# Two chained blocks on one core: weight rests on VectorE, smaller convolution pieces, an earlier bias product and a merged row scaling

## The chip, the cores and the metric

The kernel runs on one core of one Trainium2 chip. The metric is the time of one execution in microseconds (us); lower is better. Runs are summed up by their median.

## The reference

256 tokens of width 1024 go through two blocks, all in fp32. Cut to what matters here:

```
def first_block(x, ...):
    h = rms_norm(x, norm_mix_pre)
    u = h @ w_in
    o_nsa = nsa_attention(...)     # compressed, selected and window branches, with a relative bias table
    o_conv = short_conv_mixer(...)
    x = x + rms_norm(concat([o_nsa, o_conv]) @ w_out, norm_mix_post)
    h = rms_norm(x, norm_ffn_pre)
    y = (gelu(g) * up) @ w_ffn_down          # g, up: causal convolution (3 taps) of h @ w_ffn_up
    return x + rms_norm(y, norm_ffn_post)

def second_block(x, ...):
    h = concat([meta, x])                    # 16 + 256 rows
    z = rmsnorm(h, g_mix) @ w_in
    y_a = conformer_conv(conv_val, conv_gate, ...)   # 31 taps on 512 channels, layer norm, silu, @ w_conv_out
    y_b = rwkv7_mix(rwkv_in, ...)                    # a recurrence over time, 8 heads of 64, @ w_rwkv_out
    h = h + (gate_a * y_a + gate_b * y_b) @ w_o
    h = h + peer_ffn(rmsnorm(h, g_ffn), w_q, sub_keys, expert_u, expert_v)
    return rmsnorm(h, g_final)[:, N_META:]
```

## The kernel before

**Weights.** Every product is made of three matmuls (`mm3`, L371) of operands that are split into a high part and a rest. A weight tile of 128x1024 comes by a DMA on SyncE's queue into one of four `raw` buffers. ScalarE writes its high part into one of three `hl` buffers (`split`, L363); then the rest, raw minus high, is written at L364, on VectorE, or on GpSimd where the tile's `pool` flag is set in `front_tiles`. A raw buffer is free for the next load when its rest is written. `POOL1` and `POOLC` set the flag for two tiles of the first projection and four of the compression weights, and the line for `w_in_2` sets it for 35 of the 38 tiles of the second block's input projection.

**Opening** (`front_setup`, `start`, `bias_tables`). For each of two tiles of 128 rows a chain `a` or `b` makes the root of the mean square (`newton`, L421 to L429, on one number per partition), scales the rows by it and by g_pre (L797), turns them by eight TensorE transposes (L383) and splits them into hT (L805 on ScalarE, L808 on VectorE). The string `START` gives the order by hand on TensorE, VectorE, ScalarE and GpSimd: each letter takes chain a, chain b, the bias table (`t`) or a weight split (`s`) one step on.

**Boundaries** (the function around L540). Between parts the rows are normed again, in two chains: GpSimd multiplies the rows by the norm's weights (L540, two halves), `newton` runs on VectorE, and VectorE scales the product (L545, two halves); transposes follow. The steps' order is given by hand (`BORD`, `BORD1`, `BORD3`).

**Block 2.** Three generators are mixed into one TensorE order at build time. `rw`, the recurrence in five chunks of 64, sets the pace. `fill` gives projections of the next columns, so that TensorE has work while the recurrence goes through VectorE. `cf` is the conformer's convolution: four groups of 128 channels with 31 taps (L1250, L1252) on VectorE, then mean and variance by TensorE products with `cst`, the norm, the sigmoid and the split into cT. A `yield` after six taps ends a piece. The loop hands out a piece when the planned TensorE time since the start has passed CFP nanoseconds per piece given:

```
while ("U", min(ncf // 5, 3)) in emitted and (self.pe - base) > CFP * ncf:
    base = base or self.pe
    next(cf, None)
    ncf += 1
```

The products that use cT (w_conv_out) come after the recurrence. From then on block 2 has the merge with the recurrence's output oT, and after about 690 us the PEER part and the last norm follow; the change does not touch these.

Of the kernel before, what the change touches and what calls it, by code (L numbers as in the profile page):

```python
# [10 lines left out]
F32 = mybir.dt.float32  # L11
# [10 lines left out]
D = 1024  # L22
# [13 lines left out]
QUAD, PAIR = 150, 20  # L36
START = "abasabsbtasbt"
BT = (1, 2, 2, 2)
# [5 lines left out]
AC, AS, AX_, AP, AP0 = 1600, 1600, 1300, 1900, 2000  # L44
FILL0, FILL1, FILL2, CFP = 4500, .85, .7, 4900
SIDE = 2850
# [84 lines left out]
def front_tiles():  # L131

    t = []
# [52 lines left out]
    for i, c in enumerate(WIN2_ORDER):  # L186
        col("w_in_2", c, i < 3 or i >= 6)
    for name in ("w_conv_out_2", "w_rwkv_out_2"):
# [21 lines left out]
WIN_ORDER = [512, 640, 0, "k0", "k1", 128, "k2", "k3", 256, 384, 768, "v0", "v1", 1024]  # L210
POOL1 = (0, 1)
POOLC = ("k0", "k1", "v0", "v2")
for _i in range(2):
# [128 lines left out]
class Kern:  # L342
# [160 lines left out]
    def boundary(self, ys, g_post, g, hT, off, order=(0, 1), steps=BORD, lead=None, rest=None):  # L503
# [16 lines left out]
        def chain(tt):  # L520
# [17 lines left out]
            t = rows("xg")  # L538
            for c in cols:
                nc.gpsimd.tensor_mul(t[:, c], x[:, c], g[:, c])  # L540
            yield
            r = self.newton(s2, 1e-6, D)
            yield
            for c in cols:
                nc.vector.tensor_scalar(t[:, c], t[:, c], r, None, op0=OP.mult)  # L545
            parts = []
            for q in range(2):
                p = self.pb()
# [273 lines left out]
    def block1(self, ctx):  # L822
# [3 lines left out]
        self.tmp = tmp_ctx.enter_context(tc.tile_pool(name="tmp", bufs=1))  # L826
        self.g_pre = self.tmp.tile([128, 1024], F32, name="g_pre")
        nc.scalar.dma_start(self.g_pre, flat(A["norm_mix_pre"], 0, [[0, 128], [1, D]]))
        nc.scalar.dma_start(self.ident, A["cst0"])
        self.tab = self.tmp.tile([33, 8], F32, name="tab")  # L830
        nc.scalar.dma_start(self.tab, A["tab"])
        self.ohd = self.tmp.tile([33, NU], F32, name="ohd")
        nc.scalar.dma_start(self.ohd, A["ohd"])
        self.st.load()
        hT = self.turned("hT1")
# [348 lines left out]
    def block2(self, ctx):  # L1184
# [62 lines left out]
        def conformer():  # L1247
            acc = unit("acc", [128, 4, 256])
            for i in range(4):
                nc.vector.tensor_scalar(acc[:, i], UU[:, i, 46:302], self.v("cw", 120 + i), self.v("cb", i), op0=OP.mult, op1=OP.add)  # L1250
                for j in range(30):
                    nc.vector.scalar_tensor_tensor(acc[:, i], UU[:, i, 16 + j:272 + j], self.v("cw", 4 * j + i), acc[:, i],  # L1252
                                                   op0=OP.mult, op1=OP.add)
                    if j % 6 == 5:
                        yield
# [55 lines left out]
        while True:  # L1311
# [12 lines left out]
            while filled < target and fill_step():  # L1324
                pass
            while ("U", min(ncf // 5, 3)) in emitted and (self.pe - base) > CFP * ncf:
                base = base or self.pe
# [722 lines left out]
```

## Time and profile before

| | |
|---|---|
| median of 3 runs | 1519.92 us (1517.75 to 1520.23) |
| the profiled execution | 1517.68 us |
| its span, first to last instruction | 1515.9 us |
| mean granted TensorE clock | 0.978 of full speed |
| TensorE busy | 1433.8 us, 95% of the span |
| VectorE busy | 1067.5 us, 70% |
| ScalarE busy | 806.8 us, 53% |
| GpSimd busy | 282.5 us, 19% |

The profile is of one execution. Its own time stands beside the span, since sums over the trace are made against it and not against the median. PE is TensorE, DVE is VectorE, ACT is ScalarE, POOL is GpSimd, SP is SyncE; a q behind a name is the engine's queue of issues. A share of busy time is a mean over stages with different limits, so a stage is read by itself.

### The profile page before, as it was taken

To read this page: it belongs to the slowest core of one execution; us is meant where nothing else is said; L and a number is where in the kernel's file an instruction comes from. 1 tells how busy PE (TensorE), PEld (TensorE's weight loads), DVE (VectorE), ACT (ScalarE), POOL (GpSimd) and SP (SyncE) were. 2 spreads that over 40 slices of the span, in tenths; PEclk is the share of its full clock that TensorE was granted. 3 is DMA by queue.
4 is the path that set the end of the run, shared out by engine and by line. 5 is a ranking of instruction groups with operands and counts; after the bars stand their busy time and mean duration, and the time that the engine had idled before them with its cause. 6 is when DMAs were issued, how large, how long until landed. Compare 5 with 4: busy or idle time off the path is not lost.

```text
span 1515.9 us, 29516 instructions
## 1 busy us (share of the span) xinstructions
PE 1433.8 (95%) x11884; PEld 1312.1 (87%) x11884; DVE 1067.5 (70%) x1980; ACT 806.8 (53%) x1282; POOL 282.5 (19%) x143
## 2 busy tenths in 40 slices
PE   5999999997988789998999999999999999999997
PEld 4898899995877779988999899999999998888886
DVE  6877787777489974956970798874555556666666
ACT  4756565554662445544545577664444445555554
POOL 4100400005353423036786100000000000000000
PEclk9999999998998899999999999999999999999999
DMA  5634365554332112454576544457555558777773
GB/s 204 232 127 144 105 216 178 184 191 163 104 112 86 63 66 67 161 175 160 182 230 205 171 161 157 160 171 221 189 185 190 188 188 284 242 241 242 242 243 124
DMA packets 93024, 263.50 MB, mean 174 GB/s; under 512 B 10271, under 2 KB 34975, under 8 KB 92760
## 3 DMA queue, kind: packets, MB, share of 16 engines
q1 hardware_dynamic: 77200, 243.80, 49.0%
q10 hardware_dynamic: 15688, 17.83, 3.4%
q8 instruction: 93, 1.52, 0.4%
q14 instruction: 43, 0.35, 0.1%
HBM read 247.67 MB, written 13.91 MB: 173 GB/s over the span
## 4 chain that ended last, share of the span: by engine, by line
PE 75%; DVE 17%; ACT 4%; issue 2%; DMA 1%; POOL 1%; ACTq 0%; DVEq 0%; POOLq 0%
PE pb L371 39%; PE py L371 35%; DVE acc L1252 4%; DVE hl L364 2%; ACT hl L363 1%; PE pb L383 1%; DMA raw<-in_ws_dram 1%; POOL hl L364 1%; DVE m L1874 1%; DVE nc L425 0%; DVE blk L736 0%; DMA x<-in_x_dram 0%; ACT junk L515 0%; DVE nc L427 0%; DVE nc L426 0%
## 5 line engine op out<-in xcount | busy, mean ns | idle before, releaser
L371 PE MATMUL pb<-hT,hl 128*128 128x256 f32 (+1 forms) x4944 | 625.0, 285 | 9.4 <-DVE qT L364 4.0
L371 PEld LDWEIGHTS pb<-hT,hl 128*128 128x128 f32 x4944 | 607.2, 191 | 17.3 <-issue 5.1
L363 ACT ACTIVATE hl<-raw 128x1024 fp32r<-128x1024 f32 x412 | 434.1, 1054 | 231.4 <-issue 162.9
L364 DVE TENSOR_TENSOR hl<-raw,hl 128x1024 fp32r<-128x1024 f32 (+1 forms) x317 | 389.4, 1229 | 111.0 <-ACT hl L363 110.5
L371 PE MATMUL py<-hl,coef 128*128 128x512 f32 x1536 | 356.3, 390 | 0.0
L371 PEld LDWEIGHTS py<-hl,coef 128*128 128x128 f32 x1536 | 285.6, 188 | 59.3 <-ACT coef L363 0.3
L364 POOL TENSOR_TENSOR hl<-raw,hl 128x1024 fp32r<-128x1024 f32 x95 | 237.0, 2501 | 335.1 <-ACT hl L363 319.1
L1927 ACT ACTIVATE act<-pb 128x256 f32<-128x256 f32 x128 | 49.2, 384 | 166.2 <-PE pb L371 166.0
L2006 POOL TENSOR_TENSOR end<-end,end 128x512 f32<-128x512 f32 x2 | 2.6, 1278 | 664.6 <-DVE end L2004 663.1
L371 PE MATMUL py<-hT,hl 128*128 128x272 f32 (+1 forms) x768 | 118.1, 304 | 1.6 <-POOL hl L364 1.6
L371 PEld LDWEIGHTS py<-hT,hl 128*128 128x128 f32 x768 | 103.4, 198 | 8.3 <-issue 4.8
L364 DVE TENSOR_TENSOR coef<-act,coef 128x256 fp32r<-128x256 f32 x128 | 54.1, 423 | 72.3 <-ACT coef L363 72.3
L1931 DVE TENSOR_TENSOR act<-act,G 128x256 f32<-128x256 f32 x128 | 53.8, 420 | 34.1 <-ACT act L1927 33.2
L1252 DVE SCALAR_TENSOR_TENSOR acc<-UU,vt,acc 128x256 f32<-128x256 f32 x120 | 75.6, 671 | 0.7
L1887 ACT ACTIVATE G<-py 128x512 f32<-128x512 f32 x64 | 67.3, 1141 | 3.0 <-PE py L371 3.0
L1874 DVE TENSOR_TENSOR m<-e,gg 128x1536 bf16<-128x1536 bf16 x64 | 60.6, 954 | 0.7
L371 PE MATMUL py<-m,e 128*128 128x128 bf16 x768 | 52.7, 219 | 1.0 <-DVE m L1874 0.9
L363 ACT ACTIVATE coef<-act 128x256 fp32r<-128x256 f32 x128 | 51.6, 403 | 2.9 <-DVE act L1931 2.9
L1870 DVE TENSOR_TENSOR e<-gi,iota 128x1024 bf16<-128x1024 bf16 x64 | 43.7, 688 | 12.5 <-PE py L371 12.4
L371 PEld LDWEIGHTS <-e 128*128 128x128 bf16 x768 | 44.2, 97 | 4.5 <-DVE m L1874 2.5
L371 PE MATMUL py<-hl,gu 128*128 128x512 f32 x192 | 47.4, 393 | 0.4 <-DVE hl L364 0.3
L371 PEld LDWEIGHTS py<-hl,gu 128*128 128x128 f32 x192 | 34.9, 188 | 7.7 <-DVE hl L364 0.6
(419 smaller groups left out, 1358.6 us busy)
## 6 DMA issues: line engine op xcount, KB each, us to landing
raw<-in_ws_dram SPq DMA_DIRECT2D x172, 512.0 KB, 3.4
raw<-in_ut_dram SPq DMA_DIRECT2D x128, 512.0 KB, 3.4
raw<-in_ev_dram SPq DMA_DIRECT2D x128, 512.0 KB, 4.2
ad<-act ACTq DMA_DIRECT2D x90, 128.0 KB, 3.1
act<-ad SPq DMA_DIRECT2D x90, 128.0 KB, 3.0
wf<-fd ACTq DMA_DIRECT2D x2, 800.0 KB, 4.4
x<-in_x_dram SPq DMA_DIRECT2D x2, 512.0 KB, 5.9
xd<-x ACTq DMA_DIRECT2D x1, 1024.0 KB, 4.2
```

What stands on the lines that cost most here:

```text
L363: self.nc.scalar.activation(h, src, AF.Copy)
L364: (eng or self.nc.vector).tensor_sub(l, src, h.bitcast(F32))
L371: self.nc.tensor.matmul(out, lhsT, rhs, start=start, stop=stop, skip_group_check=True)
L383: self.nc.tensor.transpose(out, in_, self.ident[p0:p0 + n, p0:p0 + n])
L1252: nc.vector.scalar_tensor_tensor(acc[:, i], UU[:, i, 16 + j:272 + j], self.v("cw", 4 * j + i), acc[:, i], op0=OP.mult, op1=OP.add)
L1870: nc.vector.tensor_tensor(e.rearrange("p c a i j -> p (c a) i j"), gi[:, b].rearrange("p c (a j) -> p (c a) j", j=2)[:, :, None, :].to_bro ...
L1874: nc.vector.tensor_mul(m, e[:, 0][:, None].to_broadcast([128, 3, 2, 128, 2]), gg[:, b].rearrange("p k (a j) -> p k a j", j=2)[:, :, :, Non ...
L1887: nc.scalar.activation(G[:, :, 4 * b:4 * b + 4].rearrange("p a t -> p t a"), p.rearrange("p (t a) -> p t a", t=4), AF.Copy)
L1927: nc.scalar.activation(a, p[:, :S], AF.Gelu)
L1931: nc.vector.tensor_mul(a, a, self.G[:, c])
L2006: nc.gpsimd.tensor_mul(t[:, tt], x[:, tt, cols[1]], g[:, cols[1]])
```

## The change

1. `START` becomes another string, and the small loads of `tab` and `ohd` are issued ahead of `g_pre` and `ident` on ScalarE's queue. The bias table's products go ahead of the transposes.
2. `POOL1` and `POOLC` are empty and `w_in_2` carries no flag: 41 rests go from GpSimd to VectorE.
3. At the boundaries GpSimd's product and VectorE's scaling become one VectorE operation per half, x times r times g.
4. The conformer yields after every second tap (15 pieces for a group of channels instead of 5), and CFP goes from 4900 to 2300.

```
-START = "abasabsbtasbt"
+START = "abtabsababsts"
...
-FILL0, FILL1, FILL2, CFP = 4500, .85, .7, 4900
+FILL0, FILL1, FILL2, CFP = 4500, .85, .7, 2300
...
-        col("w_in_2", c, i < 3 or i >= 6)
+        col("w_in_2", c)
...
-POOL1 = (0, 1)
-POOLC = ("k0", "k1", "v0", "v2")
+POOL1 = ()
+POOLC = ()
...
             t = rows("xg")
-            for c in cols:
-                nc.gpsimd.tensor_mul(t[:, c], x[:, c], g[:, c])
             yield
             r = self.newton(s2, 1e-6, D)
             yield
-            for c in cols:
-                nc.vector.tensor_scalar(t[:, c], t[:, c], r, None, op0=OP.mult)
             parts = []
-            for q in range(2):
+            for q, c in enumerate(cols):
+                nc.vector.scalar_tensor_tensor(t[:, c], x[:, c], r, g[:, c], op0=OP.mult, op1=OP.mult)
...
-        self.g_pre = self.tmp.tile([128, 1024], F32, name="g_pre")
-        nc.scalar.dma_start(self.g_pre, flat(A["norm_mix_pre"], 0, [[0, 128], [1, D]]))
-        nc.scalar.dma_start(self.ident, A["cst0"])
         self.tab = self.tmp.tile([33, 8], F32, name="tab")
         nc.scalar.dma_start(self.tab, A["tab"])
         self.ohd = self.tmp.tile([33, NU], F32, name="ohd")
         nc.scalar.dma_start(self.ohd, A["ohd"])
+        self.g_pre = self.tmp.tile([128, 1024], F32, name="g_pre")
+        nc.scalar.dma_start(self.g_pre, flat(A["norm_mix_pre"], 0, [[0, 128], [1, D]]))
+        nc.scalar.dma_start(self.ident, A["cst0"])
...
-                    if j % 6 == 5:
+                    if j % 2:
                         yield
...
-            while ("U", min(ncf // 5, 3)) in emitted and (self.pe - base) > CFP * ncf:
+            while ("U", min(ncf // 15, 3)) in emitted and (self.pe - base) > CFP * ncf:
```

Three places show how the order moves. A row is line, operation, written tile, read tiles and shape; lines from about L545 on are three lower in the changed kernel.

First TensorE at its start, before: `ident` rows are the transposes of the two row tiles, `ohd,tab` the bias table's products, `hT,hl` the first projection.

```order
L383 MATMUL pb_142<-ident,xg_140 128x128 x4
L383 MATMUL pb_148<-ident,xg_140 128x128 x4
L383 MATMUL pb_174<-ident,xg_172 128x128 x4
L383 MATMUL pb_180<-ident,xg_172 128x128 x4
L371 MATMUL py_190<-ohd,tab 8x272
L371 MATMUL py_191<-ohd,tab 8x272
L371 MATMUL pb_221<-hT_0_115,hl_153 128x256 x16
```

and after the change:

```order
L371 MATMUL py_126<-ohd,tab 8x272
L371 MATMUL py_127<-ohd,tab 8x272
L383 MATMUL pb_147<-ident,xg_145 128x128 x4
L383 MATMUL pb_153<-ident,xg_145 128x128 x4
L383 MATMUL pb_174<-ident,xg_172 128x128 x4
L383 MATMUL pb_180<-ident,xg_172 128x128 x4
L371 MATMUL pb_221<-hT_0_115,hl_185 128x256 x16
```

The two bias products now lead, and the first projection follows the second tile's transposes directly.

Second, VectorE in the middle of the recurrence's set-up, before: `acc` rows are convolution taps, `iv`, `it`, `PR` and `mt` belong to the recurrence.

```order
L1488 TENSOR_TENSOR iv_4748<-iv_4748,pb_5004 128x384
L1252 SCALAR_TENSOR_TENSOR acc<-UU,vt,acc 128x256
L1541 STREAM_TRANSPOSE it_4747<-iv_4748 128x384
L1252 SCALAR_TENSOR_TENSOR acc<-UU,vt,acc 128x256 x3
L1456 TENSOR_TENSOR PR_4641<-pb_5073,cst_4086 128x256
L1457 TENSOR_TENSOR PR_4642<-pb_5073,cst_4086 128x256
L1252 SCALAR_TENSOR_TENSOR acc<-UU,vt,acc 128x256 x9
```

and after, around the same steps:

```order
L1485 TENSOR_TENSOR iv_4740<-iv_4740,pb_4990 128x384
L1249 SCALAR_TENSOR_TENSOR acc<-UU,vt,acc 128x256
L1538 STREAM_TRANSPOSE it_4739<-iv_4740 128x384
L1249 SCALAR_TENSOR_TENSOR acc<-UU,vt,acc 128x256
L1453 TENSOR_TENSOR PR_4633<-pb_5061,cst_4078 128x256
L1454 TENSOR_TENSOR PR_4634<-pb_5061,cst_4078 128x256
L1249 SCALAR_TENSOR_TENSOR acc<-UU,vt,acc 128x256
L1504 TENSOR_TENSOR AA<-AA,dc 128x1280
L1249 SCALAR_TENSOR_TENSOR acc<-UU,vt,acc 128x256
L1531 TENSOR_TENSOR mt_4736<-ac_4733,cst_4078 128x256
L364 TENSOR_TENSOR hl_5123<-raw_4689,hl_5123 128x1024
```

Long runs of taps give way to single ones, and rests (L364) stand between. From the first tap of the stage to the first state update there are 75 taps and 21 rests on VectorE in the new order, where 111 taps and no rest of `w_in_2` stood.

Third, TensorE at the end of the conformer. Before, its mean products (`acc,cst`), with a product of the recurrence and projections behind them, stand far ahead of the last state products:

```order
L371 MATMUL py_6735<-hT_0_3958,hl_6568 128x256
L371 MATMUL py_6744<-acc,cst_4086 128x256 x4
L371 MATMUL pb_6750<-ZZ,inv 64x128 x8
L371 MATMUL py_6735<-hT_0_3958,hl_6568 128x256
L371 MATMUL py_6735<-hT_1_3959,hl_6568 128x256
```

After, with the last state products 32 rows ahead of this:

```order
L371 MATMUL py_6989<-hT_0_3954,hl_6786 128x256
L371 MATMUL py_7031<-UU,cst_4078 128x256 x2
L383 MATMUL pb_6970<-ident,O 64x128 x4
L383 MATMUL pb_6977<-ident,O 64x128 x4
L371 MATMUL py_7031<-UU,cst_4078 128x256 x2
L371 MATMUL py_7075<-cT_7050,hl_6886 128x256
```

The variance products (`UU,cst`) now stand directly ahead of the products that use cT, with only the transposes of O between. The mean products stand 12 rows further up, with 15 projections behind them and 27 ahead, back to the last state products.

## Rows read from the trace of the kernel before

**Rows 1.** The page: busy time by engine, and the chain that ended last by engine.
```profile
PE 1433.8 (95%) x11884; PEld 1312.1 (87%) x11884; DVE 1067.5 (70%) x1980; ACT 806.8 (53%) x1282; POOL 282.5 (19%) x143
...
PE 75%; DVE 17%; ACT 4%; issue 2%; DMA 1%; POOL 1%; ACTq 0%; DVEq 0%; POOLq 0%
```

**Rows 2.** Groups by line and shape: busy us, mean ns | idle before.
```profile
L364 DVE TENSOR_TENSOR hl<-raw,hl 128x1024 fp32r<-128x1024 f32 x314 | 386.6, 1231 | 110.9 <-ACT hl L363 110.5
L364 POOL TENSOR_TENSOR hl<-raw,hl 128x1024 fp32r<-128x1024 f32 x95 | 237.0, 2501 | 335.1 <-ACT hl L363 319.1 <-PE py L371 8.2 <-DVE cv L1140 3.6
L545 DVE TENSOR_SCALAR xg<-xg,nc 128x512 f32<-128x512 f32 x12 | 5.4, 489 | 0.5
```

**Rows 3.** Timeline of the opening: start us, length us, engine, line, operation.
```profile
0.73 0.41 ACTq L828 DMA_DIRECT2D g_pre<-in_norm_mix_pre_dram  x1
...
8.32 0.16 DVE L427 SCALAR_TENSOR_TENSOR nc<-nc,nc 128x1 f32<-128x1 f32 x1
...
10.79 2.38 DVE L425 SCALAR_TENSOR_TENSOR nc<-nc,nc 128x1 f32<-128x1 f32 x1
10.80 2.35 POOL L364 TENSOR_TENSOR hl<-raw,hl 128x1024 fp32r<-128x1024 f32 x1 [4.85 <-ACT hl L363]
...
13.40 2.35 DVE L427 SCALAR_TENSOR_TENSOR nc<-nc,nc 128x1 f32<-128x1 f32 x1
...
16.23 1.42 DVE L797 SCALAR_TENSOR_TENSOR xg<-x,nc,g_pre 128x512 f32<-128x512 f32 x2
...
17.04 1.97 PE L383 MATMUL pb<-ident,xg 128*128 128x128 f32 x8 [5.30 <-DVE xg L797]
...
20.85 11.04 PE L371 MATMUL pb<-hT,hl 128*128 128x256 f32 x72
```

**Rows 4.** Windows: length, busy PE, PEld, DVE, ACT, POOL, PEclk, DMA share, GB/s.
```profile
400.66:548.07 147.41, 121.01 (x2216) 108.90 (x2215) 132.41 (x210) 70.46 (x121) 60.36 (x25) 0.91 0.25 84
548.07:559.57 11.50, 11.37 (x141) 10.19 (x143) 8.73 (x17) 3.48 (x8) 2.65 (x1) 0.85 0.14 47
559.57:607.56 47.99, 47.67 (x696) 42.93 (x692) 20.37 (x41) 27.17 (x51) 14.18 (x6) 1.00 0.20 67
```

**Rows 5.** VectorE's groups by shape, 400.66 to 548.07 us.
```profile
L1252 DVE SCALAR_TENSOR_TENSOR acc<-UU,vt,acc 128x256 f32<-128x256 f32 x111 | 69.2, 668 | 0.4
...
L1463 DVE TENSOR_TENSOR K<-K,SQ 128x1088 f32<-128x1088 f32 x1 | 3.5, 3450 | 0.0
...
L1444 DVE COPY dc<-L 128x20 f32<-128x20 f32 x1 | 2.0, 1965 | 0.0
...
L1438 DVE TENSOR_TENSOR AA<-AA,KN 128x1280 f32<-128x1280 f32 x1 | 1.5, 1480 | 0.0
```

**Rows 6.** Timeline at 497 us: nine taps in a row.
```profile
497.44 3.64 DVE L1252 SCALAR_TENSOR_TENSOR acc<-UU,vt,acc 128x256 f32<-128x256 f32 x9
```

**Rows 7.** The page: DMA issues, KB each, median us to landing.
```profile
x<-in_x_dram SPq DMA_DIRECT2D x2, 512.0 KB, 5.9
```

**Rows 8.** Timeline of boundary 3.
```profile
663.90 2.49 POOL L540 TENSOR_TENSOR xg<-x,grow 128x512 f32<-128x512 f32 x2
...
667.51 2.79 PE L371 MATMUL py<-hl,hT 128*128 128x256 f32 x12 [2.42 <-DVE hT L558]
```

**Rows 9.** Timeline of the conformer's end, 594 to 613 us.
```profile
594.52 1.97 PE L371 MATMUL py<-UU,cst 128*128 128x256 f32 x8
...
597.44 1.75 DVE L1269 RECIPROCAL rv<-rv 128x256 f32<-128x256 f32 x1 [0.48 <-ACT rv L1268]
...
601.47 2.07 ACT L1273 ACTIVATE UU<-acc,vt 128x256 f32<-128x256 f32 x4
...
607.36 1.06 ACT L363 ACTIVATE cT<-acc 128x1024 fp32r<-128x1024 f32 x1 [0.44 <-DVE acc L1275]
...
607.56 5.24 PE L371 MATMUL py<-hT,hl 128*128 128x256 f32 x42
...
612.64 6.09 PE L371 MATMUL py<-cT,hl 128*128 128x256 f32 x50
```

## The prediction

> **What bounds the kernel now.** I read the page first. TensorE is busy 95% of the span and holds 75% of the chain that ended last; VectorE holds 17%, GpSimd 1% [rows 1]. So only time in which TensorE stands still, or has its clock lowered, can be won. GpSimd's small share of the chain hides how it acts. The changed line L364 has two prices: a rest of 128x1024 takes 1.23 us on VectorE and 2.50 us on GpSimd [rows 2]. And GpSimd's rests stop VectorE. In the timeline of the opening, L425 and L427 handle one number per partition: L427 takes 0.16 us alone, but 2.35 us at 13.40, and L425 takes 2.38 us from 10.79, where a GpSimd rest starts at 10.80 and takes 2.35 [rows 3]. The small operation ends with the rest. That is what to see there: a GpSimd rest can cost VectorE its own whole length.
>
> Then I asked by stage. In block 2 from 400.66 to 548.07 us VectorE is busy 132.4 of 147.4 us, TensorE only 121.0, at a mean granted clock of 0.91 of 2.4 GHz [rows 4]. This is the one long stage in which TensorE is not the limit; from 559.57 on it is busy 47.67 of 47.99 us at full clock. What VectorE is busy with there is partly waiting: 111 taps (L1252) average 0.668 us, while nine taps in a row take 3.64, or 0.40 each [rows 5, 6]. Seven larger operations, from L1463 (3.45 us) to L1444 (1.97), are prolonged too; a like one undisturbed takes 1.48 (L1438) [rows 5].
>
> **Part 1: opening, and rests of block 1 on VectorE.** The second tile's norm chain loses about 2.2 us at L425 and 2.2 at L427 [rows 3]; both rests behind these stalls leave GpSimd. So its last step (L797, now 16.23) starts near 11.9, or near 12.0 with one small delay. Now the transposes (17.04, 1.97 us) start at once, and the two bias-table products, which filled 19.01 to 20.85, stand ahead of all transposes where TensorE is idle anyway. The first projection starts at 20.85 now. I put it at 12.0 + 0.8 (first half of L797) + 1.97 + about 0.4 for the ScalarE copy = 15.2, that is 5.7 earlier. It needs a first VectorE rest (1.23) ahead of it; this fits behind L797. On ScalarE's queue g_pre is now issued behind two small loads; at 0.41 us an issue it goes out at 1.6 instead of 0.73, and even with the 5.9 us of a 512 KB load it lands at 7.5, before the first chain's statistic is ready (L427 ends at 8.48) [rows 3, 7]. Later GpSimd rests no longer hold up the compression products (a gain), but raw tiles are freed later, as the first rest moves behind the chain, and the loads into them with it (a loss). I take **−5.5 us**, between −1 (loads decide) and −7.
>
> **Part 2: boundaries.** A chain loses two GpSimd products and two VectorE scalings (0.49 each), and gets two VectorE operations that read two tiles and a scale. L797 is of that kind: 1.42 for two, 0.71 each, so +0.22 each [rows 2, 3]. At boundary 3 the GpSimd product (663.90, 2.49 us) lies over the norm chain, and TensorE waits 2.42 us for the VectorE steps behind it [rows 8]: I take −2.0 there. The two others show the same sequence, and I give each −1, the middle of 0 and −2. Together **−4 us**, between −1 and −6.
>
> **Part 3: block 2's stage.** Out of VectorE's 132.4 us go: 69.2 − 111 × 0.40 = 24.8 us by which taps are prolonged; for the seven large operations some 12.3 us; and 36 taps that the new order puts off to later (111 now, 75 then), 36 × 0.40 = 14.4. Into it come 21 rests at 1.14 (1.23 less the overlap of neighbours) = 24. That leaves about 105 us. TensorE's own floor is 121.0 × 0.91 = 110 us at full clock [rows 4]. The stage now takes 147.4 at a VectorE busy share of 0.90. With two engines at 105 and 110 and chains that go back and forth between them, I take the same 0.89 of the longer: 110 / 0.89 = 124, so **−23 us**, between −15 (share 0.83) and −32 (0.95). Behind it, 548.07 to 559.57 runs at 0.85; full clock would save 11.37 × 0.15 = **1.7 us** [rows 4].
>
> The Trainium skill's "SBUF — State Buffer", section "Who interferes with whom", says that whichever of the two engines starts first holds the shared port for its whole instruction and the other fully blocks. By that rule GpSimd's 60 us in the stage [rows 4] would all be VectorE's loss, not the 37 that the prolonged operations show; the stage would then lie at TensorE's floor, and the sum 9 us lower. I go by the rows, since the rest of the 60 us lies where no VectorE operation is prolonged.
>
> **Part 4: what the smaller pieces cost later.** A piece is due whenever TensorE's time since the start of the convolution passes CFP for each piece given. 20 pieces × 4900 = 98,000 ns become 60 × 2300 = 138,000 ns: the conv ends some 40 us of TensorE time later. So 45 of 120 taps lie behind 548 (9 now). There VectorE is busy 8.73 + 20.37 = 29.1 of 59.5 us [rows 4]; with 36 more taps at 0.45 (16), nine rests at 1.14 (10), and without the conformer's end (some 6, below), it comes to about 50. TensorE is the limit there and the scan's steps leave VectorE waiting, so most is hidden; I take **+2 us**, between 0 and +8.
>
> The conformer's own end (mean product, variance, reciprocal, sigmoid, split into cT) falls behind the last state products. Now those products end near 607.56, 42 projections follow, and cT is ready before 612.64, when it is used [rows 9]. In the new order no projection is left between the variance products and cT. From the last state product: 27 projections 3.4 (27/42 × 5.24); mean products 1.9 (priced as the variance products, 1.97); subtraction 1.2; square 1.06; variance products 1.97 with eight transposes of O between, 1.0; two short steps 0.8; reciprocal 1.75; multiply 1.2; sigmoid 2.07; multiply 1.2; ScalarE's hi part 1.06 [rows 9], with a VectorE pass over 128x1024 priced as the rest [rows 2]. That is 18.6, and the VectorE order puts the group norm of O, two rests and the oc products in between, some 4: 22.7. cT is due at 612.64 − 607.56 = 5.1 now. Of the 17.6 later, 3.9 are products that no longer stand ahead and 1.0 transposes that no longer stand behind: **+13 us**, between +8 and +18.
>
> Such a gap may also lower the clock behind it. The stage ahead of 548 has TensorE idle for 26 us, and the stretch after it, though busy, was granted 0.85 [rows 4]; the same loss behind the new gap is **+1.7**. The Trainium skill ("TensorE: Matmul & The Clock Gate", section "HAM oscillation — how this bites in real kernels") tells of a matmul stream that starts cold after each wait for data. If that does not hold here, the sum is 1.7 us lower; no run here shows it for this gap yet.
>
> **Sum:** −5.5 − 4 − 23 − 1.7 + 2 + 13 + 1.7 = −17.5. The profiled execution took 1517.68 us (span 1515.9), so 1500.2; the median of the three runs lies 2.2 above it, so **1502 us**. The rest of the program (from some 690 us) is unchanged.
>
> **Rivals.**
> - *Better: GpSimd blocked more than the rows admit.* Stage at 115 (−32), tail +8, the others as above: 9 and 5 below the forecast's −17.5, so −31.5, 1488 us; with opening −7 and boundaries −6, 1485. For it: L425 and L427 stall for the rest's full length [rows 3]. Against: TensorE's floor of 110 and chains between. Chance 0.17. The rule of "SBUF — State Buffer" in the Trainium skill would bring this case about.
> - *The tail eats most.* Stage −15, tail +18, opening −5.5, boundaries −4, scan +2: about −5, 1515 us. For it: the new stage has almost equal loads on both engines. Chance 0.17.
> - *The opening doesn't come earlier*, since raw tiles are freed later and loads decide: +4.5 on the forecast, 1506 us. Against: the chain of waits has DMA at 1% [rows 1]. Chance 0.06.
> - *Slower: VectorE becomes the limit of the scan stage.* VectorE is in order; a tap or rest ahead of a state update delays TensorE's next state product. Deciding point: VectorE's load from 548 to 607 over about 55 of 59 us; then its overrun lies on the path. With +12 there, the stage only −8, tail +18, opening and boundaries −9.5: about +12, 1532 us. For it: 50 of 59 is my own estimate. Against: the scan's operations now wait for TensorE. Chance 0.08.
> - Forecast: 0.52, its own range 1494 to 1510.
>
> **Numbers.** A measurement here can tell about 0.2%, 3 us. The range 1485 to 1518 leaves out the slower rival and the ends of the tail and of the better case. Faster by over 0.2% (under 1516.9): all but the slower rival and a third of the tail's case, 0.86; the same 0.06; slower 0.08.
>
> **What would show it.** Right: L425 and L427 of the second chain at 0.2 us and the first projection near 15; no L364 on GpSimd between 400 and 550; taps near 0.45 us mean; the stage some 20 us shorter with a higher granted clock; and a wait of TensorE of 10 us or more for cT about 25 us behind the last state product. Wrong: TensorE waiting for L364 on VectorE or for raw loads in the opening; waits for state updates between 548 and 607; or cT ready without a gap, in which case the time is nearer to 1488.

## The result and the profile after

The changed kernel took 1496.07 us, the median of four runs (1494.59 to 1499.52), beside 1519.59 us before: a ratio of 0.985, 95% interval 0.9831 to 0.987, or 23.5 us less. The forecast was 1502 us, 17.5 us less. The profiled execution took 1499.52 us with a span of 1497.7; it is the slowest of the four, and the one of before is the fastest of its four, so the two traces show 18.2 us of the gain. A second profile of the same kernel, below, has a span of 1490.4.

The page after, with the lines that answer to [rows 1, 2]:

```profile
PE 1426.8 (95%) x11884; PEld 1306.0 (87%) x11884; DVE 1062.1 (71%) x2021; ACT 802.1 (54%) x1279; POOL 161.1 (11%) x90
...
PE 85%; DVE 7%; ACT 3%; DMA 3%; issue 1%; POOL 1%; ACTq 0%; DVEq 0%; POOLq 0%
...
L364 POOL TENSOR_TENSOR hl<-raw,hl 128x1024 fp32r<-128x1024 f32 x54 | 132.6, 2461 | 196.0 <-ACT hl L363 177.0
...
L1249 DVE SCALAR_TENSOR_TENSOR acc<-UU,vt,acc 128x256 f32<-128x256 f32 x120 | 52.8, 482 | 0.5
```

VectorE's part of the chain that ended last fell from 17% to 7%. It took over 41 rests, some 50 us, and is busy 5 us less: the same 120 taps took 75.6 us before and 52.8 now.

To say where the time went, the second block is cut at events that both kernels have: the first product of `LW` with `wup`, the first state product, the last one, and the first product of oT. Windows before and after; columns as in [rows 4].

```profile
397.22:569.79 172.57, 146.04 (x2475) 130.75 (x2476) 142.92 (x231) 83.11 (x146) 68.16 (x28) 0.91 0.25 82
569.79:607.63 37.84, 37.52 (x599) 34.17 (x595) 19.17 (x38) 21.38 (x39) 11.82 (x5) 1.00 0.21 71
607.63:625.58 17.95, 17.44 (x148) 17.27 (x147) 17.00 (x35) 9.68 (x15) 0.00 (x0) 1.00 0.45 148
```

```profile
393.69:540.16 146.47, 140.18 (x2476) 126.21 (x2477) 127.38 (x241) 79.26 (x143) 1.17 (x1) 0.95 0.29 95
540.16:573.98 33.82, 33.60 (x583) 30.95 (x579) 24.78 (x51) 14.87 (x30) 0.00 (x0) 1.00 0.29 96
573.98:608.91 34.93, 22.96 (x162) 21.50 (x163) 24.36 (x43) 15.94 (x23) 0.00 (x0) 0.85 0.18 61
```

Up to the first cut the change is 3.5 us ahead. The stage in front of the state products is 26.1 us shorter, the state products 4.0, and the part behind them 17.0 us longer. From oT to the last transposes of boundary 3 (670.94 before, 650.67 after) it wins 3.6 us, and the rest of the program loses 2.1. The sum is −3.5 − 26.1 − 4.0 + 17.0 − 3.6 + 2.1 = −18.1.

The 3.5 us are those of two single executions. Counting the runs below, the program of before was profiled three times up to that cut, with the same order on every engine, and reached it at 397.22, 401.01 and 395.79 us; the changed program was profiled four times and reached it at 393.69, 389.46, 390.99 and 387.24 us. The means are 398.0 and 390.3, 7.7 us apart, and a single profile can lie 3 us off.

The stage of the prediction has other cuts: it starts with VectorE's first scan (L1405 before, L1402 now), at 400.66 us before, and ends with the last `inv`, a step of the recurrence's set-up on VectorE (L1573 before, L1570 now), at 548.07 us before. The windows after with the prediction's cuts, beside [rows 4]:

```profile
397.13:520.05 122.92, 116.63 (x2216) 105.70 (x2215) 105.60 (x191) 66.59 (x118) 1.17 (x1) 0.94 0.29 96
520.05:530.79 10.74, 10.74 (x155) 9.51 (x154) 10.68 (x26) 3.48 (x8) 0.00 (x0) 1.00 0.31 99
530.79:573.98 43.19, 42.97 (x665) 39.11 (x665) 34.15 (x74) 20.74 (x42) 0.00 (x0) 1.00 0.26 88
```

The opening, in the timeline after, beside [rows 3]:

```profile
1.80 0.37 ACTq L829 DMA_DIRECT2D g_pre<-in_norm_mix_pre_dram  x1
...
6.24 1.97 PE L371 MATMUL py<-ohd,tab 33*8 33x272 f32 x4 [6.24 <-DMA ohd<-in_ohd_dram]
...
9.77 1.42 DVE L794 SCALAR_TENSOR_TENSOR xg<-x,nc,g_pre 128x512 f32<-128x512 f32 x2 [2.74 <-DMA g_pre<-in_norm_mix_pre_dram]
...
11.59 0.22 DVE L425 SCALAR_TENSOR_TENSOR nc<-nc,nc 128x1 f32<-128x1 f32 x1
...
12.04 0.16 DVE L427 SCALAR_TENSOR_TENSOR nc<-nc,nc 128x1 f32<-128x1 f32 x1
...
13.49 1.97 PE L383 MATMUL pb<-ident,xg 128*128 128x128 f32 x8 [0.17 <-DVE xg L794]
...
16.00 8.73 PE L371 MATMUL pb<-hT,hl 128*128 128x256 f32 x72 [0.54 <-DVE hT L805]
```

L425 and L427 of the second chain take 0.2 us now, not 2.4, the bias products lead, and the first projection starts at 16.00 instead of 20.85. A new wait is there as well: VectorE stands 2.74 us for g_pre.

VectorE's groups in the stage, after (393.69 to 540.16 us), beside [rows 5]:

```profile
L1249 DVE SCALAR_TENSOR_TENSOR acc<-UU,vt,acc 128x256 f32<-128x256 f32 x105 | 45.6, 481 | 0.1
L364 DVE TENSOR_TENSOR hl<-raw,hl 128x1024 fp32r<-128x1024 f32 x25 | 30.6, 1223 | 3.9 <-ACT hl L363 3.8
...
L1460 DVE TENSOR_TENSOR K<-K,SQ 128x1088 f32<-128x1088 f32 x1 | 1.3, 1283 | 0.0
...
L1441 DVE COPY dc<-L 128x20 f32<-128x20 f32 x1 | 0.2, 181 | 1.0 <-ACT L L1431 1.0
```

The operations that stood for up to 3.45 us have their own length back, and 25 rests have joined them.

What TensorE waited for in the stage before, the longest wait and the only one for GpSimd (columns: us in total, times, longest):

```profile
PE pb L1565 <- DVE it L1541: 7.2, 1, 7.2
...
PE py L371 <- POOL hl L364: 1.6, 1, 1.6
```

All waits for VectorE there make 24.9 us, so GpSimd's slower rests cost TensorE little directly. After the change no wait for VectorE is left among those over half a microsecond.

The conformer's end after, beside [rows 9]:

```profile
573.91 3.46 PE L371 MATMUL py<-hT,hl 128*128 128x256 f32 x27
...
577.20 1.89 PE L371 MATMUL py<-acc,cst 128*128 128x256 f32 x8
...
583.73 1.03 PE L371 MATMUL py<-UU,cst 128*128 128x256 f32 x4
...
587.34 1.74 DVE L1266 RECIPROCAL rv<-rv 128x256 f32<-128x256 f32 x1
...
590.79 2.08 ACT L1270 ACTIVATE UU<-acc,vt 128x256 f32<-128x256 f32 x4 [1.35 <-DVE acc L1268]
...
594.61 1.06 ACT L363 ACTIVATE cT<-acc 128x1024 fp32r<-128x1024 f32 x1 [1.74 <-DVE acc L1272]
...
595.71 2.70 PE L371 MATMUL py<-cT,hl 128*128 128x256 f32 x9 [10.95 <-ACT cT L363]
```

TensorE waits 10.95 us for cT, in one piece, 21.7 us behind the last state product (573.98). Before, cT was used 5.0 us behind it and nothing waited. VectorE is not late: the last tap ended at 551.3 us, 26 us ahead of the mean products. What moved is the place of the mean products in TensorE's order, from 17.8 us ahead of the last state product's end to 3.2 behind it.

Boundary 3 after, beside [rows 8]:

```profile
648.55 1.81 PE L371 MATMUL py<-hl,hT 128*128 128x256 f32 x12 [0.36 <-DVE hT L555]
```

TensorE's wait for hT is 0.36 us instead of 2.42.

One place went the other way, ahead of boundary 1. Four rests of the feed-forward's first tiles are still on GpSimd (three are shown):

```profile
145.23 2.61 DVE L1026 TENSOR_SCALAR P<-P,su 128x128 f32<-128x128 f32 x2
145.41 7.01 POOL L364 TENSOR_TENSOR hl<-raw,hl 128x1024 fp32r<-128x1024 f32 x3 [129.88 <-ACT hl L363]
...
147.90 0.33 PE L383 MATMUL pb<-ident,P 128*128 128x128 f32 x1 [2.00 <-DVE P L1026]
```

The second of the two L1026 operations starts when GpSimd's rest runs and ends with it; TensorE waits 2.00 us. In the profiled execution of before, the same operation started 0.2 us ahead of GpSimd's rest and had its own length. It is a race: of the ten profiles that keep these rests on GpSimd, the operation was held in six and slipped through in four, on both sides of the change.

### The profile page after: what moved, and what is told of

The parts are those of the page before. It is cut to its first block, busy times and chain, and to the rows that moved or that the text cites. A ratio compares the mean times of both kernels' runs of the same rounds, so it can differ in the third digit from the quotient of the medians.

```text
span 1497.7 us, 29472 instructions
## 1 busy us (share of the span) xinstructions
PE 1426.8 (95%) x11884; PEld 1306.0 (87%) x11884; DVE 1062.1 (71%) x2021; ACT 802.1 (54%) x1279; POOL 161.1 (11%) x90
## 4 chain that ended last, share of the span: by engine, by line
PE 85%; DVE 7%; ACT 3%; DMA 3%; issue 1%; POOL 1%; ACTq 0%; DVEq 0%; POOLq 0%
PE pb L371 42%; PE py L371 40%; DVE hl L364 1%; PE pb L383 1%; DMA raw<-in_ws_dram 1%; POOL hl L364 1%; PE pb L1370 1%; ACT hl L363 1%; DVE m L1871 1%; DMA wf<-fd 1%; DMA g_pre<-in_norm_mix_pre_dram 1%; DMA cst<-in_cst_dram 0%; DVE nc L428 0%; ACT junk L515 0%; ACT last L363 0%
## 5 line engine op out<-in xcount | busy, mean ns | idle before, releaser
L371 PEld LDWEIGHTS pb<-hT,hl 128*128 128x128 f32 x4944 | 604.9, 190 | 16.3 <-issue 7.4
L364 DVE TENSOR_TENSOR hl<-raw,hl 128x1024 fp32r<-128x1024 f32 (+1 forms) x358 | 439.7, 1228 | 122.1 <-ACT hl L363 120.0
L364 POOL TENSOR_TENSOR hl<-raw,hl 128x1024 fp32r<-128x1024 f32 x54 | 132.6, 2461 | 196.0 <-ACT hl L363 177.0
L371 PE MATMUL py<-hT,hl 128*128 128x272 f32 (+1 forms) x768 | 112.0, 299 | 0.0
L364 DVE TENSOR_TENSOR coef<-act,coef 128x256 fp32r<-128x256 f32 x128 | 54.1, 423 | 72.2 <-ACT coef L363 72.2
L1928 DVE TENSOR_TENSOR act<-act,G 128x256 f32<-128x256 f32 x128 | 53.9, 421 | 33.5 <-ACT act L1924 32.9
L371 PE MATMUL py<-m,e 128*128 128x128 bf16 x768 | 52.8, 219 | 1.0 <-DVE m L1871 0.9
L1249 DVE SCALAR_TENSOR_TENSOR acc<-UU,vt,acc 128x256 f32<-128x256 f32 x120 | 52.8, 482 | 0.5
L1867 DVE TENSOR_TENSOR e<-gi,iota 128x1024 bf16<-128x1024 bf16 x64 | 43.7, 689 | 12.5 <-PE py L371 12.4
L371 PEld LDWEIGHTS py<-hl,gu 128*128 128x128 f32 x192 | 34.9, 188 | 7.6 <-DVE hl L364 0.5
```

The lines of the kernel that those rows point to most:

```text
L364: (eng or self.nc.vector).tensor_sub(l, src, h.bitcast(F32))
L371: self.nc.tensor.matmul(out, lhsT, rhs, start=start, stop=stop, skip_group_check=True)
L1867: nc.vector.tensor_tensor(e.rearrange("p c a i j -> p (c a) i j"), gi[:, b].rearrange("p c (a j) -> p (c a) j", j=2)[:, :, None, :].to_bro ...
L1928: nc.vector.tensor_mul(a, a, self.G[:, c])
```

## Experiments

Theory G: GpSimd's rests stop VectorE's operations on SBUF, and the change wins what that waiting cost. Theory P, its rival for block 2: the pieces of two taps win, since the recurrence's steps no longer stand behind runs of six. Theory T: the late cT is a net loss, and the pieces with CFP 2300 should be taken back. Rival D: taps that come back ahead of the state products cost what T would win.

### The four parts alone

Each was put into the kernel before. The opening: `START`, the order of the small loads, and

```
-POOL1 = (0, 1)
-POOLC = ("k0", "k1", "v0", "v2")
+POOL1 = ()
+POOLC = ()
```

> The kernel before with the opening alone (START, the order of the small loads, POOL1 and POOLC empty). My theory: the changed kernel's first projection starts some 4.9 us earlier, and of this some 3 to 4 us are left behind the compression, so 3 to 5 us faster (ratio 0.9967 to 0.998). Rival: the loads and the late g_pre eat it, within 1 us of before.

The boundaries (L540 and L545 become one VectorE step):

> The kernel before with the boundaries alone (one VectorE step, no GpSimd product). My theory: 3 us at boundary 3 and under 1 us at the two others, so 2 to 4 us faster. Rival: the GpSimd product stood beside other work and the dearer VectorE step costs what it saves, 0 to 1 us.

The rests:

```
-        col("w_in_2", c, i < 3 or i >= 6)
+        col("w_in_2", c)
```

> The kernel before with the 35 rests of w_in_2 moved to VectorE alone; pieces of six taps and CFP 4900 stay, so the conformer ends early and cT is ready. Theory G (GpSimd rests block VectorE's taps): taps fall from 0.67 to under 0.5 us each, the stage from 400 to the end of the scan is 20 us or more shorter, and without the late cT the whole is 20 to 30 us faster, better than the changed kernel's rests and pieces together. Theory P (the small pieces free the recurrence's steps from runs of taps): under 10 us faster.

The pieces:

```
-                    if j % 6 == 5:
+                    if j % 2:
...
-FILL0, FILL1, FILL2, CFP = 4500, .85, .7, 4900
+FILL0, FILL1, FILL2, CFP = 4500, .85, .7, 2300
...
-            while ("U", min(ncf // 5, 3)) in emitted and (self.pe - base) > CFP * ncf:
+            while ("U", min(ncf // 15, 3)) in emitted and (self.pe - base) > CFP * ncf:
```

> The kernel before with pieces of two taps and CFP 2300 alone; the rests stay on GpSimd. Theory G: the taps stay prolonged (over 0.6 us), the stage gains under 10 us by 36 taps put off, and cT comes late by 11 us or more: 2 us faster to 12 us slower. Theory P: 15 us or more off the stage, so faster on the whole in spite of the late cT.

| part alone | median us | ratio to before (1518.87 us), 95% interval |
|---|---|---|
| opening | 1511.47 | 0.9956 (0.9936 to 0.9976) |
| boundaries | 1511.36 | 0.9961 (0.9938 to 0.9984) |
| rests | 1506.32 | 0.9921 (0.9894 to 0.9948) |
| pieces | 1533.18 | 1.0111 (1.0079 to 1.0143) |

The windows of the rests alone, cut at the same four events:

```profile
398.93:549.50 150.57, 138.96 (x2478) 123.30 (x2479) 132.07 (x249) 80.02 (x143) 1.17 (x1) 0.97 0.29 96
549.50:589.50 40.00, 39.84 (x616) 36.21 (x612) 28.33 (x53) 23.23 (x41) 0.00 (x0) 1.00 0.19 60
589.50:607.58 18.08, 15.31 (x128) 14.95 (x128) 15.44 (x34) 8.63 (x13) 0.00 (x0) 1.00 0.46 164
```

And of the pieces alone:

```profile
395.79:562.79 167.00, 145.74 (x2475) 130.87 (x2476) 141.67 (x231) 83.55 (x146) 67.08 (x28) 0.92 0.25 85
562.79:602.89 40.10, 36.55 (x583) 33.22 (x579) 14.99 (x30) 15.07 (x30) 11.83 (x5) 0.91 0.21 67
602.89:637.95 35.06, 23.07 (x163) 21.62 (x163) 24.71 (x44) 15.96 (x23) 0.00 (x0) 0.85 0.22 75
```

with the taps' group on the page:

```profile
L1252 DVE SCALAR_TENSOR_TENSOR acc<-UU,vt,acc 128x256 f32<-128x256 f32 x120 | 68.4, 618 | 0.7
```

The stage is 22.0 us shorter with the rests alone, and nothing behind it is longer by more than 2.2. With the pieces alone TensorE's load, VectorE's load and the stage's length are those of the opening alone (166.91 us, next rows), which has pieces of six; the taps stay at 0.62 us. Theory P falls for the pieces alone. The late cT is there in full: 35.06 us where 17.95 stood.

The whole gain by the rests was 12.0 us, less than the 20 to 30 that I expected. Of the 22.0 us in this trace 16.1 are left at the program's end (1.7 are lost ahead of the first cut, 2.3 between the first state product and oT, 1.9 behind it), the profiled execution is the fastest of the six, and against the shorter course shown below the stage is only 16.3 us shorter.

The 17 us lost by the pieces alone are more than the 12 that theory G allowed: it let the stage gain by taps put off, but all 120 taps ran ahead of the first state product, 111 of them ahead of the last `inv`, as before. In the changed kernel 71 do. So the pieces put taps off only together with the moved rests. The mean products come 3.2 us behind the last state product all the same, though the last tap ended 50 us ahead of it.

Opening and boundaries each measured more than expected (6.7 and 5.9 us by the ratios, where 3 to 5 and 2 to 4 were expected), and more than their places show. A part of it lies in the stage of block 2, whose code neither touches. The opening alone, and a second profile of the kernel before (below):

```profile
395.36:562.27 166.91, 145.47 (x2476) 130.57 (x2476) 141.55 (x231) 83.24 (x146) 67.31 (x28) 0.92 0.26 85
```

```profile
401.01:573.42 172.41, 146.28 (x2476) 131.13 (x2476) 143.01 (x231) 83.19 (x146) 68.82 (x28) 0.91 0.24 82
```

The order of each engine is the same in both. GpSimd's timeline shows where they part. In the first profile of before:

```profile
429.49 2.60 POOL L364 TENSOR_TENSOR hl<-raw,hl 128x1024 fp32r<-128x1024 f32 x1 [2.42 <-ACT hl L363]
432.94 2.84 POOL L364 TENSOR_TENSOR hl<-raw,hl 128x1024 fp32r<-128x1024 f32 x1 [0.85 <-ACT hl L363]
435.96 3.39 POOL L364 TENSOR_TENSOR hl<-raw,hl 128x1024 fp32r<-128x1024 f32 x1 [0.18 <-ACT hl L363]
```

and with the opening alone:

```profile
427.97 2.41 POOL L364 TENSOR_TENSOR hl<-raw,hl 128x1024 fp32r<-128x1024 f32 x1 [2.77 <-ACT hl L363]
431.04 6.60 POOL L364 TENSOR_TENSOR hl<-raw,hl 128x1024 fp32r<-128x1024 f32 x2 [0.66 <-ACT hl L363]
```

Counted from the first `LW` product, VectorE's and GpSimd's operations up to there lie within 0.04 us of each other; then the first of these rests starts at 32.27 in the one and 32.61 in the other. From there on GpSimd's rests lie differently against VectorE's operations, and 130 us later the stage is 5.7 us longer or shorter. The boundaries alone and the pieces alone took the shorter course too (166.98 and 167.00). For the pieces that settles something: from the program's start to 60 us into the stage, where no tap has run yet, their order is that of the kernel before on every engine, and yet the courses part. So one order can take either course.

In the opening's profile 5.7 us are this, and it is 1.9 us ahead at the first cut, which is inside the scatter of that cut. The boundaries have 3.4 us between oT and boundary 3, the same 5.6, and 6.1 us at the first cut, of which the scatter cannot be taken off. How much of the two medians is their own stays open.

### The kernel before again

> The kernel before once more, for a second profile. In the first its stage from 447.6 to the first state product took 122.2 us, but 115.1 in three kernels that have the same code there. If the place where GpSimd's rests fall against VectorE's operations varies, this profile shows 115 to 122 with VectorE's taps differing in mean length, and the same number of taps. If it is always 122, an earlier part of the program sets it.

Its median is 1519.46 us, ratio 0.9999 (0.9979 to 1.002). The stage took 172.41 us, as in the first profile (172.57), with 143.01 us of VectorE beside 142.92, so both profiles of this kernel took the longer course. What decides between the courses is not shown; two profiles cannot tell whether this kernel sometimes takes the shorter one. The place ahead of boundary 1 differs between the two: here L1029 was held as L1026 above, TensorE waited 2.0 us for it, and boundary 1 came 3.7 us later than in the first profile of the same kernel.

### The changed kernel, with the pieces taken back in two ways

These three, and the run with `LEADP` empty below, ran on one chip beside the kernel before (1516.15 us).

> The changed kernel once more, for comparison with the other runs on this chip and for a second profile of it. Expected: 22 to 25 us faster than before, TensorE's wait for cT 10 to 12 us again. If the opening's late g_pre was chance, it is gone or smaller here.

CFP alone:

```
-FILL0, FILL1, FILL2, CFP = 4500, .85, .7, 2300
+FILL0, FILL1, FILL2, CFP = 4500, .85, .7, 1630
```

> The changed kernel with CFP 1630 instead of 2300: the same pieces of two taps are due over 97,800 ns of TensorE time as the pieces of before, so the conformer ends before the last state products. Theory T (the late cT is a net loss): TensorE's wait for cT of 11 us goes, and the stage grows by less than that, so 5 to 13 us faster than the changed kernel. Rival D (the 36 taps that come back load VectorE where it limits): the stage from 445 to the first state product grows by 8 us or more, and the whole is within 3 us of the changed kernel.

All of part 4 undone (`j % 6 == 5`, `ncf // 5`, CFP 4900):

> The changed kernel with the pieces of before (six taps, CFP 4900): every part but the pieces. Theory T: cT is not late, the stage is some 6 us longer than the changed kernel's, so 4 to 10 us faster than the changed kernel. Rival D: the stage is 12 us or more longer, and the whole no faster.

| kernel | median us | ratio to before | stage | state products | to oT |
|---|---|---|---|---|---|
| changed, again | 1495.37 | 0.9876 (0.9846 to 0.9907) | 144.84 | 33.82 | 35.80 |
| CFP 1630 | 1502.63 | 0.9918 (0.9888 to 0.9948) | 154.44 | 50.24 | 15.79 |
| six taps, CFP 4900 | 1495.52 | 0.9874 (0.9843 to 0.9905) | 152.31 | 40.07 | 18.08 |

The last three columns are the profiles' windows in us. The changed kernel was 20.8 us under before by the medians, where 22 to 25 were expected. The wait for cT came again, 11.0 us. The late g_pre was not chance: VectorE waited 2.64 us for it again and the first projection started at 15.91. TensorE's transposes waited for `ident` (3.2 us), which is issued behind g_pre.

With six taps, the rows are

```profile
387.24:539.55 152.31, 141.38 (x2478) 125.54 (x2479) 132.00 (x249) 80.02 (x143) 1.17 (x1) 0.94 0.29 95
539.55:579.62 40.07, 39.89 (x616) 36.27 (x612) 28.34 (x53) 23.20 (x41) 0.00 (x0) 1.00 0.19 61
579.62:597.70 18.08, 15.31 (x129) 14.96 (x128) 15.44 (x34) 8.62 (x13) 0.00 (x0) 1.00 0.47 162
```

and the sum of the three, 210.5 us, is 4 us under the changed kernel's 214.5 and 215.2. Two runs below have the same code from the first cut on: the changed kernel with `LEADP` empty has 217.5, six taps without any rest of the first block on GpSimd 213.2. So six taps are some 4 us shorter here, with a scatter of 3. The medians do not tell the two apart. Both T and D have their share. The late cT costs 17 us; in return the stage is 6 to 7.5 us shorter, as VectorE is loaded 4.6 us less there (7 taps and a rest fewer), and the state products 6.2, of which 3.9 are the mean and variance products that moved. By the windows T was right in sign and too high in size; the medians show no gain, as D had it for the whole. The pieces that cost 17 us in the kernel before cost nothing by the medians where the rests are on VectorE, so the parts do not add up: alone they make 6.7 + 5.9 + 12.0 − 16.9 = 7.7 us, together 22.8 by the same measure.

CFP 1630 is slower than the changed kernel (all six of its times lie above all six of that kernel on the same chip), which neither theory gave. Here cT is ready so early that many of its 96 products become fillers among the state products (677 matmuls in that window, 616 with six taps), and only 67 matmuls are left between the last state product and oT (128 with six taps). Waits of TensorE in the run with CFP 1630, 395 to 625 us:

```profile
PE pb L371 <- ACT oT L363: 3.8, 1, 3.8
PE pb L383 <- DVE O L1599: 3.5, 1, 3.5
PE py L371 <- ACT cT L363: 2.4, 1, 2.4
```

TensorE waits for the recurrence's own output, where w_conv_out's products had covered it. So cT can be too early as well as too late.

### The rests of the first block

```
-LEADP = (0, 1, 2, 3)
+LEADP = ()
```

> The changed kernel with LEADP empty: the rests of the four tiles that lead the first block's feed-forward product also go to VectorE. In the changed kernel one of them, on GpSimd from 145.4 us, stopped VectorE's L1026 and TensorE waited 2.0 us for it. Theory G: that wait goes, 1 to 3 us faster than the changed kernel. Rival: four rests of 1.23 us in VectorE's way at boundary 1 cost as much.

1491.37 us, 0.9835 (0.9803 to 0.9867), 4.0 us under the changed kernel on the same chip, though the intervals overlap. TensorE waited 0.8 us for L1026 instead of 2.2, and the last transposes of boundary 1 came at 167.32, with 173.01 and 169.06 in the changed kernel's two profiles. But the run with six taps, which keeps the four rests on GpSimd, came there at 165.79: the wait is mostly gone, a gain in time is not shown.

All rests of the first block on VectorE, with pieces of six (`FGP, FUP = (), ()` and `FLP = ()` besides):

> The changed kernel with pieces of six taps and CFP 4900, and with LEADP, FGP, FUP and FLP empty, so that no rest of the first block stays on GpSimd. If a rest on GpSimd costs VectorE where the two run side by side, this is 3 to 8 us faster than the run with six taps alone, and GpSimd's rests are gone from 145 to 360 us. Rival: rests on VectorE delay the boundary's chain, no change within 2 us.

1492.07 us, 0.9824 (0.9798 to 0.985), where the run with six taps alone had 0.9874 on another chip. GpSimd's rests are gone up to boundary 3, and TensorE's wait for `gu` at the end of the feed-forward is 1.1 us where the changed kernel has 2.7 and 0.6. The expected 3 to 8 us are there by the medians (3.4 us) and by the ratios (7.6 us), but the intervals overlap a little.

### `LEADP` empty, with CFP 1750 and 1850

Between CFP 1630 and 2300 lies a value at which the variance products stand ahead of the last state products, and the products of cT behind them. `LEADP = ()` is taken along.

```
-LEADP = (0, 1, 2, 3)
+LEADP = ()
...
-FILL0, FILL1, FILL2, CFP = 4500, .85, .7, 2300
+FILL0, FILL1, FILL2, CFP = 4500, .85, .7, 1750
```

> The changed kernel with LEADP empty and CFP 1750: the conformer's mean products come ahead of the last state products, and cT is used behind them, as in the kernel before. If the late cT costs 16.7 us and fewer taps in the stage and shorter scan give 13 back, this lies 2 to 6 us under the changed kernel with LEADP empty. Rival (taps that come back into the stage cost as much as in the run with CFP 1630): equal to it or up to 5 us slower.

> As the one with CFP 1750, but CFP 1850: variance products right behind the last state products, some 40 projections between them and cT. Wait for cT some 5 to 8 us instead of 11; the time between that with CFP 1750 and the changed kernel with LEADP empty.

With CFP 1750 the median is 1488.72 us, 0.9802 of before (0.9776 to 0.9828), which was 1519.27 us on this chip; the interval lies under those of the changed kernel (0.9831 to 0.987, and 0.9846 to 0.9907 again) and of six taps. Against the nearest rival, `LEADP` empty with CFP 2300 (0.9803 to 0.9867), the intervals overlap, so the 2 to 6 us expected of CFP 1750 itself are not shown. With CFP 1850 it is 1492.93 us, 0.9823 (0.9795 to 0.9852). The windows of CFP 1750:

```profile
388.40:539.90 151.50, 143.03 (x2487) 127.39 (x2488) 131.45 (x246) 79.83 (x143) 1.17 (x1) 0.94 0.29 96
539.90:577.36 37.46, 36.58 (x588) 32.90 (x584) 25.02 (x50) 19.02 (x35) 0.00 (x0) 1.00 0.19 58
577.36:598.55 21.19, 18.10 (x147) 17.30 (x146) 19.97 (x41) 12.79 (x20) 0.00 (x0) 1.00 0.45 149
```

The part behind the state products is 21.2 us instead of 34.9, at full clock. The three windows make 210.2 us, 4 to 5 under the changed kernel. With CFP 1850 the wait for cT is 6.3 us and the sum 214.8, no better than with 2300.

## Why the prediction was right, point by point

The sign, the range (1485 to 1518) and the mechanism hold; the gain was 23.5 us where 17.5 were forecast. Times of the trace below are of the first profiles before and after.

- **GpSimd stops VectorE.** Shown by the rests alone: the same taps in the same pieces go from 75.6 to 54.5 us, and the seven larger operations go from 20.5 to 7.9 in the changed kernel, 12.5 us where the forecast had 12.3. For the taps it took 24.8 us; 22.8 were measured. They do not come down to 0.40 each: the 71 in the stage take 31.5 us, 0.44 each.
- **The opening, −5.5.** The first projection came 4.85 us earlier, not 5.7. The step that was mis-sized is g_pre: I let it land at 7.5, by the median of another load; it was used at 9.77, eight microseconds behind its issue. At the attention's first product the lead was 5.8 us, near the forecast; of this 1.5 was left at boundary 1, behind the GpSimd rest that held L1026, and 3.5 at the first cut (7.8 in the second profile). Opening and the first two boundaries together were forecast at 7.5 up to that cut, and the means of the profiles there are 7.7 us apart.
- **The boundaries, −4.** Boundary 3 gave 3.6 us where 2.0 were taken; the two others cannot be read under the scatter ahead of boundary 1.
- **The stage, −23.** At the forecast's own cuts it gave 24.5 us, from 147.4 to 122.9. VectorE's load there is 105.6 us, forecast some 105. TensorE's 116.63 us at a clock of 0.94 are 109.6 at full clock, forecast 110, and 109.6 of 122.92 is the share of 0.89 that was taken. 21 rests came in, as forecast. Of the taps 40 were put off and not 36: 111 stood ahead of the last `inv` before, and 71 do now, 75 with the four first operations (L1247), which the 111 leaves out. The counts given with the change go to this `inv`; ahead of the first state update (`S`) there were 120 taps and are 86. Small errors cancel in the sum: taps and rests are dearer (0.44 and 1.22 us, not 0.40 and 1.14), the other operations win 14.8 us and not 12.3.
- **The luck in it.** Both profiles of before took the longer of two courses through the stage. The forecast did not know of the other; against it, the way up to the first state product is 20.4 us shorter, not 26.1, and the stretch behind the last `inv` was granted 1.00 already (9.96 us with the opening alone).
- **Behind the stage, −1.7 and +2.** From 548.07 to the last state product the change won 5.6 us. 3.9 of it are the mean and variance products, which the forecast books with the late cT. The other 1.7 are the clock: TensorE was granted 0.85 in the first stretch before, and 1.00 now. The +2 did not come: TensorE is busy 53.7 of 53.9 us although 49 taps and nine rests run there.
- **The late cT, +13, and the clock behind it, +1.7.** cT was expected 22.7 us behind the last state product and came after 21.7. The part to oT is 17.0 us longer; without the 3.9 us of products that moved there it is 13.1, where the two terms made 14.7. Behind the gap the 96 products of cT took 13.36 us and not 6.09 + 5.71 = 11.8, with a granted clock of 0.85 in the window: 1.6 us, as forecast. The forecast put the delay down to a convolution that ends later. The taps do end closer to the last state product (22.7 us ahead, not 50.5), but they are done 26 us before the mean products, and with the pieces alone they end as early as before and cT comes as late. It is the order on TensorE that delays cT.
- **The rivals.** The better case, by which GpSimd's 60 us would all come back, did not come: up to the first state product VectorE's load fell by 15.5 us with 30.6 us of rests added, so 46 us were won, 7 of them by the 15 taps still put off at that point. The other 39 stand against 68 us of GpSimd. GpSimd's rests were prolonged as well (2.60, 2.84 and 3.39 us in the rows above, 2.41 for one that was not), which fits GpSimd waiting in its turn. The slower case, VectorE as the limit among the state products, did not come near: from 520.05 to the last state product VectorE is busy 44.8 of 53.9 us (10.68 + 34.15), where the deciding point was 55 of 59.

Against the profiled gain of 18.2 the forecast's 17.5 is near. Ahead of the first cut 4.0 us less was won than forecast, and 2.1 were lost behind boundary 3; the stage gave 1.5 more, the +2 that did not come 2.0, the late cT 1.6, boundary 3 1.6. The two losses are inside the scatter of single profiles: the changed kernel's second profile, with a span 25.5 us under that of before, is 7.8 us ahead at the first cut, has a stage 1.6 us shorter and loses nothing behind boundary 3. The median's further 5 us lie in this scatter. The 1488 us that the prediction named for a kernel without the gap is also the median with CFP 1750, but that kernel has four rests less on GpSimd besides, so the agreement proves little.

## What to carry to other kernels

An engine that is 19% busy can be the limit of another one: compare the mean length of an operation with its length when it runs alone, and look at what runs on the other engine at that moment. Work that is given out in smaller pieces also moves what stands behind its last piece in the other engines' orders; follow it to whoever needs its result, and set the spacing so that this is done neither after its user nor so early that its user fills the wrong gap. Parts of a change need not add up: the pieces cost 17 us without the moved rests and nothing with them. And where two engines race for one thing, one order of operations can take two courses, here 5.7 us apart, and places far ahead of a stage can scatter by several microseconds. So single parts must be judged by windows of more than one trace, and not by their time alone.

## What the runs showed of the hardware that was not expected

- Operations that read a single SBUF tensor are held too: a copy of 20 numbers per partition took 1.97 us beside a GpSimd rest and 0.18 without, and L1026, a multiplication by one number per partition, ended with the rest that ran beside it. The Trainium skill's "SBUF — State Buffer", section "Who interferes with whom", counts copies and such scalings among the operations that can take the shared port; these rows agree.
- Block 2's stage with the same order on all engines ran 172.57 and 172.41 us in two profiles (before), 166.91 and 166.98 in two others (opening alone, boundaries alone): two courses, with nothing between in these four. A fifth (pieces alone, the same order for the first 60 us) took 167.00.
- The load of g_pre, issued at 1.80 instead of 0.73 us, held VectorE until 9.77 us, where 8.96 had been early enough before. Four weight loads of 512 KB are issued on SyncE's queue from 1.66 us on; whether they delay it was not tried.
